# RWKV inverse in a two-layer hybrid block: its DRAM trips issued by ScalarE into ScalarE's own DMA queue

## The chip, the cores and the metric

The kernel runs on one core of one Trainium2 chip. The metric is the device time of one execution in microseconds, the median of three runs. TensorE multiplies (PE in the profile, its weight loads PEld), VectorE (DVE), ScalarE (ACT) and GpSimd (POOL) work element by element, and SyncE (SP) here only issues DMAs. DMAs that one engine issues go through a queue of that engine. Sixteen DMA engines move the data.

## The reference, cut to what matters

Two layers on 512 tokens of width 1024, each a half-step feed-forward, a mixer of three branches (retention, sparse attention, RWKV-7) merged by gates, and a second half-step feed-forward. The change touches the RWKV-7 branch alone, eight heads of 64, whose state is updated token by token:

```python
def step(S, inp):
    r_t, w_t, k_t, v_t, kk_t, a_t = inp
    sa = jnp.einsum('bhvk,bhk->bhv', S, -kk_t)
    S = S * w_t[:, :, None, :] + sa[..., None] * (kk_t * a_t)[:, :, None, :] + v_t[..., None] * k_t[:, :, None, :]
    return S, jnp.einsum('bhvk,bhk->bhv', S, r_t)
```

The kernel computes this in chunks of 64 tokens. In each chunk and head the dependence of later tokens on earlier ones is a triangular system (I - N) X = I of size 64, and its inverse is what the DRAM trips serve.

## The kernel before, in words

**Dense products.** A weight tile of 512 columns (a slot, 256 KB) is loaded by SP into `raw` (L54, four buffers), split by ACT into `whi` (L49) and by DVE into `wlo` (L50), three buffers each, and used by twelve matmuls of 512 columns, in three passes (L109, L111, L113). SP also moves saved tiles of 256 KB to and from DRAM (`th` at L863, `y` at L856, L908 and others), in the same queue.

**The mixer.** `Rwkv.pairs` walks through the four head pairs of a layer. For each pair `next` calls `front2` (decay, keys, operands `st` and `bk`) and `mid` (chunk products and inverse); `chain` then carries the state over eight chunks and `post` normalises. All of that is a serial chain with the highest priority, level `rec`. TensorE's time between its steps is filled by `K.fill(n, after)`: it traces n products of the queued dense work (retention, attention, gates, merging, the next pair's projections) and puts them, on TensorE, behind the instruction `after`. So the order on TensorE is mostly written out by hand: FV = 38 products behind `self.gate`, then the first small matmul `pace` (L470) that follows four steps of the inverse, then FP (11 to 15) products behind each further `pace`, FD = 29 behind the last, then the joining matmuls (L487, L492). The order on the other engines comes from a planner, which simulates the program's time and queues each instruction on its engine where it is ready. At run time every engine, and every DMA queue's issuer, takes its instructions in that fixed order and waits at the head of its line.

**The trips in `mid`.** (1) `zb` (L426, DVE, four parts) is the masked product. Its diagonal 32x32 blocks go to DRAM scratch `dn` in four DMAs (L456, 32 KB each, runs of 128 bytes). (2) One DMA (L457) brings `dn` back as `N`, one instance a partition, four times over (512 KB, the leading dimension of its source is a broadcast of four). (3) One DMA (L461) loads the start value `X` (`idg`, into buffer `cum`). (4) POOL runs 31 steps of two instructions (L466, L468). (5) X goes to DRAM scratch `dx` (L473) and comes back in four DMAs as `mt` (L479), is transposed by DVE into `m1` (L480), and the joining matmuls (L487) follow. There are eleven DMAs a pair and eight pairs, four in each layer.

Of the kernel before, what the change touches and what calls it, by code (L numbers as in the profile page):

```python
# [7 lines left out]
P = 128  # L8
# [6 lines left out]
T = 512  # L15
# [6 lines left out]
class Core:  # L22
# [17 lines left out]
    def ps(self, tag="f"):  # L40
        """one PSUM bank: d for the dense products, r for the recurrence, f for the rest."""
        return self.psp.tile([P, T], F32, tag=tag, name=self.nm("ps" + tag), bufs={"d": 4, "r": 2, "f": 2}[tag])
# [4 lines left out]
    def split(self, x, hi, lo):  # L47
        """exact parts of float32 for the one-pass products: x = hi + lo."""
        self.nc.scalar.activation(hi, x, AF.Copy)  # L49
        self.nc.vector.tensor_tensor(out=lo, in0=x, in1=hi.bitcast(F32), op=ALU.subtract)  # L50
# [6 lines left out]
    def wslot(self, src, n):  # L57
        """n <= 512 weight columns a partition, split."""
        raw = self.early.popleft() if self.early else self.load(src, n)
        hi = self.wp.tile([P, T], F32R, tag="whi", name=self.nm("whi"), bufs=3)  # L60
        lo = self.wp.tile([P, T], F32R, tag="wlo", name=self.nm("wlo"), bufs=3)
        with self.at("split"):
            self.split(raw[:, :n], hi[:, :n], lo[:, :n])
        return hi, lo

    @contextmanager
    def at(self, level):
        """what is traced here takes its place in that level of the scheduler's order."""
        s, self.tc.cur_priority = self.tc.cur_priority, self.level[level]
        yield  # L70
        self.level[level], self.tc.cur_priority = self.tc.cur_priority, s

    def fill(self, n=None, after=None):
        """trace n products of the queued work, on the tensor engine behind `after`; n None: all that is urgent."""
        with ExitStack() as es:
            es.enter_context(self.at("norm"))
            if after:
                es.enter_context(self.tc.issue_after(after.ins))
            while n != 0 and (self.urgent or n):
                g = self.urgent[0] if self.urgent and self.between else self.work  # L80
                try:
                    new = next(g)
                except StopIteration:
                    if g is self.work:
                        break
                    self.urgent.popleft()
                    continue
                if g is self.work:
                    self.between = new
                if new == "wait":  # L90
                    break
                if n and not new:
                    n -= 1
# [11 lines left out]
    def mm3(self, out, a, b, start, stop):  # L105
        """three passes: hi*hi + hi*lo + lo*hi; a is stationary."""
        nc = self.nc
        (ah, al), (bh, bl) = a, b
        nc.tensor.matmul(out, ah, bh, start=start, stop=False)  # L109
        yield  # L110
        nc.tensor.matmul(out, ah, bl, start=False, stop=False)  # L111
        yield
        nc.tensor.matmul(out, al, bh, start=False, stop=stop)  # L113
        yield

    def dense(self, w, x):
        """w [128, K, 128] in DRAM, x: K split chunks of the transposed input -> PSUM [128 features, 512 tokens]."""
        yield True
        pt = self.ps("d")
        n = len(x)  # L120
        for s0 in range(0, n, 4):
            nk = min(4, n - s0)
            hi, lo = self.wslot(w[:, s0:s0 + nk, :].rearrange("p k f -> p (k f)"), nk * P)
            for k in range(nk):
                f = slice(k * P, k * P + P)
                yield from self.mm3(pt, (hi[:, f], lo[:, f]), x[s0 + k], s0 + k == 0, s0 + k == n - 1)
        return pt

    def dense_tok(self, w, n, evac):
        """w [128, 8, n] in DRAM -> evac(token tile, PSUM [128 tokens, n features])."""  # L130
        yield True
        pts = [self.ps("d") for _ in range(4)]
        for k in range(KC):
            hi, lo = self.wslot(w[:, k, :], n)
            xh, xl = self.xg[k]
            for t in range(4):
                f = slice(t * P, t * P + P)
                yield from self.mm3(pts[t][:, :n], (xh[:, f], xl[:, f]), (hi[:, :n], lo[:, :n]), k == 0, k == KC - 1)
        for t in range(4):
            evac(t, pts[t][:, :n])  # L140
# [13 lines left out]
    def prep(self, x, c, gi, p):  # L154
        """chunk c of x^T -> split x*g, and its squares into the running sum."""
# [19 lines left out]
    def rstd(self, p, keep=True):  # L175
        """1/rms of each token: rs [128, 4] on the tokens' partitions, rb [128, 512] on every partition."""
# [17 lines left out]
    def ffn(self, xT, w_in, w_out, out_cb, done):  # L194
        """w_in [44, 128, 8, 128], w_out [8, 128, 22, 128]; x += 0.5 * swiglu, then out_cb(chunk)."""
        nc, tc = self.nc, self.tc
        with tc.tile_pool(name=self.nm("ffn"), bufs=1, reuse_waits="tile") as fp:
            tl = lambda tag, bufs=1, dt=F32: fp.tile([P, T], dt, tag=tag, name=self.nm(tag), bufs=bufs)
            act = []
            for j in range(NF):  # L200
# [6 lines left out]
                nc.gpsimd.tensor_tensor(out=u, in0=s, in1=u, op=ALU.mult)      # 2 * silu(g) * u  # L207
# [11 lines left out]
# columns of the rwkv parameter tile  # L219
MU, W0, A0, KK, KA, RK, LNW, LNB, NPAR = 0, 14, 18, 22, 26, 30, 34, 38, 42  # L220

# products traced behind the steps of a pair: its mixing products, the way to DRAM, four steps of the inverse, the way
# back, the joining of its blocks, each step of the chain, the chain; FM: behind no step
# [6 lines left out]
class Rwkv:  # L230
    """One layer's RWKV-7 branch, head pair by head pair (heads 2p at partitions 0-63, 2p+1 at 64-127)."""

    def __init__(self, K, pool, par, w2a2, g2, cst, y_out):
# [6 lines left out]
        # both low-rank factors: one's high parts at its rows, its low parts at the other's  # L240
# [9 lines left out]
        self.hwa = self.t("hwa", [P, 8])     # w0/2, a0/2  # L250
# [21 lines left out]
    def wide(self, h, ch):  # L272
        """columns ch of a low-rank factor's product with its half of la."""
        nc, s, z = self.nc, slice(64 * h, 64 * h + 64), self.K.ps("r")
        nc.tensor.matmul(z, self.wa[h][:, ch], self.lh[h], start=True, stop=False)
        nc.tensor.matmul(z, self.wa[h][s, ch], self.ll[s], start=False, stop=True)
        return z

    def shift(self, b, ps, out):
        """token shift of one projected block (still without its rstd) into out."""  # L280
# [25 lines left out]
    def front(self, p, blk):  # L306
        """projections of pair p; blk(b) gives the PSUM tile of projected block b."""
# [31 lines left out]
    def front2(self, p, r, k, v):  # L339
# [5 lines left out]
        # decay  # L345
# [15 lines left out]
        # in-context rate  # L361
# [6 lines left out]
        # normalised key  # L368
# [16 lines left out]
        # bonus  # L385
# [10 lines left out]
        # b (times -2)  # L396
# [12 lines left out]
    def mid(self, d):  # L409
        """chunk products, the triangular inverses, token-major operands."""  # L410
# [17 lines left out]
        with self.tc.issue_after(zl.ins):  # L428
            # token-major b|k and v
# [20 lines left out]
        # diagonal 32x32 blocks, one instance a partition  # L450
        dn = K.dram([4, 8, 32, 32], "dn", 2)
        N = self.t("N", [P, 32, 32])
        for h in range(2):
            for b in range(2):
                src = zb[64 * h + 32 * b:64 * h + 32 * b + 32, :, 64 * h + 32 * b:64 * h + 32 * b + 32]
                nc.sync.dma_start(dn[2 * h + b].rearrange("c s t -> s c t"), src)  # L456
        nc.sync.dma_start(N, dn.rearrange("b c s t -> (b c) s t")[None].to_broadcast([4, 32, 32, 32]))  # L457
        # X = (I - N)^-1; partition group g has the rows 4i+g
        X = self.t("cum", [P, 8, 32])
        tmp = self.t("E", [P, 8 * 31])  # L460
        nc.sync.dma_start(X, c["idg"])  # L461
# [11 lines left out]
        nc.sync.dma_start(dx.rearrange("b c (i g) t -> g (b c) i t", g=4), X)  # L473
        mt = d["mt"] = self.t("mt", [P, 8, 64])
        m1 = self.t("m1", [P, 8, 32])
        for h in range(2):
            a = 64 * h
            for b in range(2):
                nc.sync.dma_start(mt[a + 32 * b:a + 32 * b + 32, :, 32 * b:32 * b + 32], dx[2 * h + b].rearrange("c s t -> s c t"))  # L479
# [92 lines left out]
class Ret:  # L572
    """One layer's retention, two heads (a quarter) at a time; 128-token chunks are the token tiles."""
# [8 lines left out]
    def quarter(self, q, w):  # L582
        """w [128, 8, 512]: columns q (2x64), k (2x64), v (2x128)."""
# [28 lines left out]
    def heads(self, q, X, kd):  # L612
        K, nc, c = self.K, self.nc, self.c
        # states after chunks 0..2
# [60 lines left out]
class Dsa:  # L675
    """One layer's sparse attention: index scores, exact top-128, masked softmax over the causal keys."""
# [7 lines left out]
    def parts(self, pt, h, tag):  # L684
        """rows 64h.. of pt, split, on both halves of the partitions."""
# [9 lines left out]
    def stack(self, pt):  # L695
        """for each half of pt's rows, the high parts in their place and the low parts on the other half."""
# [10 lines left out]
    def dot(self, out, q, k, h):  # L707
        """q stacked (hi at half h), k in parts: hi*hi + lo*hi, then hi*lo."""
# [4 lines left out]
    def rope(self, x, nh, t):  # L713
        """first 16 of each head's 64 columns; x [128, nh, 64]."""
# [8 lines left out]
    def index(self, w):  # L723
        """w [128, 8, 452]: dk 64 | ki 64 | qi 256 | dv 64 | wi 4."""
# [52 lines left out]
    def attend(self, w):  # L777
        """w [128, 8, 512]: dq."""
# [12 lines left out]
        for qt in range(4):  # L791
# [6 lines left out]
            for b in range(4):  # L798
# [12 lines left out]
                # both heads' weights, transposed and split, against v's parts side by side  # L811
# [29 lines left out]
def gate(K, w, tl):  # L841
    """tanh(z / 2) and z of one gate block z."""
# [7 lines left out]
def gates(K, l, pool, a, yret, yg, thd):  # L850
    """the gated retention output, and tanh of the first len(thd) merge gates, to DRAM."""
# [14 lines left out]
def merge(K, l, pool, mh, a, yd, thd, rw):  # L866
    """sum over branches of sigmoid(gate) * (y @ p), times 2."""
# [159 lines left out]
def consts():  # L1027
# [19 lines left out]
    rel=p[None,:]-p[:,None]      # i - j, rows j  # L1047
# [9 lines left out]
def layout(i):  # L1057
    """the inputs re-laid for the chip: weights in tiles, vectors by partition, x transposed."""
# [39 lines left out]
```

## Time and profile before

| | us |
|---|---|
| median of 3 runs (lowest, highest) | 3109.18 (3108.01, 3110.92) |
| span of the profiled execution | 3103.6 |
| median less span | 5.6 |
| TensorE busy | 2990.3 (96%) |
| VectorE busy | 1761.8 (57%) |
| ScalarE busy | 1081.5 (35%) |
| GpSimd busy | 715.2 (23%) |

The span reaches from the first to the last instruction of one profiled execution. Busy time is a union of instructions, and a matmul's end is modelled. SP has no busy time in this profile: it only waits and issues.

### The profile page before, as it was taken

To read this page: it belongs to the slowest core of one execution; us is meant where nothing else is said; L and a number is where in the kernel's file an instruction comes from. 1 tells how busy PE (TensorE), PEld (TensorE's weight loads), DVE (VectorE), ACT (ScalarE), POOL (GpSimd) and SP (SyncE) were. 2 spreads that over 40 slices of the span, in tenths; PEclk is the share of its full clock that TensorE was granted. 3 is DMA by queue.
4 is the path that set the end of the run, shared out by engine and by line. 5 is a ranking of instruction groups with operands and counts; after the bars stand their busy time and mean duration, and the time that the engine had idled before them with its cause. 6 is when DMAs were issued, how large, how long until landed. Compare 5 with 4: busy or idle time off the path is not lost.

```text
span 3103.6 us, 40717 instructions
## 1 busy us (share of the span) xinstructions
PE 2990.3 (96%) x14336; PEld 2373.5 (76%) x14336; DVE 1761.8 (57%) x3641; ACT 1081.5 (35%) x1892; POOL 715.2 (23%) x1186
## 2 busy tenths in 40 slices
PE   9999999999899999999999999999999899999998
PEld 7888877767667778888888888677776677788886
DVE  5443388758675675443344433887585746644433
ACT  4333343334333233333333333433333333333322
POOL 2110024342433031111011101243423340311100
PEclk9999999999899999999999999899999999999999
DMA  4223422223223452233322234222333135523232
GB/s 136 98 97 106 117 72 70 73 85 124 81 85 96 139 190 95 95 99 94 97 95 97 98 109 118 66 72 71 96 110 92 64 110 155 175 92 99 96 95 89
DMA packets 203580, 314.08 MB, mean 101 GB/s; under 512 B 46320, under 2 KB 60400, under 8 KB 203376
## 3 DMA queue, kind: packets, MB, share of 16 engines
q1 hardware_dynamic: 203376, 311.49, 32.2%
q8 instruction: 112, 1.84, 0.2%
q14 instruction: 92, 0.75, 0.1%
HBM read 277.86 MB, written 33.55 MB: 100 GB/s over the span
## 4 chain that ended last, share of the span: by engine, by line
PE 74%; DVE 10%; POOL 6%; DMA 6%; issue 3%; ACT 1%; SPq 0%; DVEq 0%; POOLq 0%; ACTq 0%
PE psd L113 22%; PE psd L109 22%; PE psd L111 22%; DMA N<-dn 3%; POOL cum L468 2%; POOL E L466 2%; DVE wlo L50 2%; PE psr L421 1%; DMA th<-th 1%; PE psr L504 1%; PE psf L96 1%; DMA dx<-cum 1%; DMA y<-y 1%; DVE cb L523 1%; PE psr L514 1%
## 5 line engine op out<-in xcount | busy, mean ns | idle before, releaser
L49 ACT ACTIVATE whi<-raw 128x512 fp32r<-128x512 f32 (+2 forms) x920 | 571.5, 622 | 1259.6 <-PE psd L111 927.2
L50 DVE TENSOR_TENSOR wlo<-raw,whi 128x512 fp32r<-128x512 f32 (+2 forms) x920 | 657.6, 715 | 560.0 <-ACT whi L49 543.9
L111 PE MATMUL psd<-xl,whi 128*128 128x512 f32 x2144 | 856.0, 399 | 2.4 <-DVE xl L161 2.4
L109 PE MATMUL psd<-xh,whi 128*128 128x512 f32 x2144 | 850.6, 397 | 1.5 <-DVE g L203 1.5
L113 PE MATMUL psd<-xh,wlo 128*128 128x512 f32 x2144 | 849.9, 396 | 0.1
L111 PEld LDWEIGHTS psd<-xl,whi 128*128 128x128 f32 x2144 | 406.7, 190 | 88.9 <-DVE xl L161 4.4
L109 PEld LDWEIGHTS psd<-xh,whi 128*128 128x128 f32 x2144 | 406.6, 190 | 88.5 <-issue 3.4
L113 PEld LDWEIGHTS psd<-xh,wlo 128*128 128x128 f32 x2144 | 406.9, 190 | 84.1 <-issue 1.4
L207 POOL TENSOR_TENSOR u<-s,u 128x512 f32<-128x512 f32 x88 | 141.2, 1605 | 841.0 <-DVE u L206 726.3
L109 PE MATMUL psd<-ah,whi 128*128 128x512 f32 x704 | 277.4, 394 | 0.0
L113 PE MATMUL psd<-ah,wlo 128*128 128x512 f32 x704 | 276.0, 392 | 0.0
L111 PE MATMUL psd<-al,whi 128*128 128x512 f32 x704 | 273.2, 388 | 0.0
L172 POOL TENSOR_TENSOR sq<-sq,sq 128x512 f32<-128x512 f32 x42 | 56.1, 1336 | 467.4 <-ACT sq L170 467.4
L113 PE MATMUL psd<-whi,xl 128*128 128x512 f32 (+1 forms) x384 | 160.6, 418 | 0.0
L111 PE MATMUL psd<-wlo,xh 128*128 128x512 f32 (+1 forms) x384 | 156.1, 407 | 0.0
L113 PEld LDWEIGHTS psd<-ah,wlo 128*128 128x128 f32 x704 | 132.1, 188 | 31.0
L109 PE MATMUL psd<-whi,xh 128*128 128x512 f32 (+1 forms) x384 | 155.1, 413 | 0.0
L111 PEld LDWEIGHTS psd<-al,whi 128*128 128x128 f32 x704 | 132.2, 188 | 29.6
L109 PEld LDWEIGHTS psd<-ah,whi 128*128 128x128 f32 x704 | 132.3, 188 | 26.3
L50 DVE TENSOR_TENSOR al<-u,ah 128x512 fp32r<-128x512 f32 x88 | 61.8, 702 | 153.6 <-ACT ah L49 153.4
L206 DVE TENSOR_TENSOR u<-psd,rb 128x512 f32<-128x512 f32 x88 | 60.9, 692 | 127.3 <-PE psd L113 127.3
L810 POOL TENSOR_SCALAR L<-L,mx 128x128 f32<-128x128 f32 (+3 forms) x64 | 71.4, 1118 | 199.4 <-DVE mx L809 99.0
(262 smaller groups left out, 3907.2 us busy)
## 6 DMA issues: line engine op xcount, KB each, us to landing
raw<-in_wf_dram SPq DMA_DIRECT2D x184, 256.0 KB
raw<-in_ffa_in_dram SPq DMA_DIRECT2D x176, 256.0 KB
raw<-in_ffb_in_dram SPq DMA_DIRECT2D x176, 256.0 KB
th<-th SPq DMA_DIRECT2D x96, 256.0 KB
raw<-in_ffa_out_dram SPq DMA_DIRECT2D x80, 256.0 KB
raw<-in_wt_dram SPq DMA_DIRECT2D x80, 256.0 KB
raw<-in_ffb_out_dram SPq DMA_DIRECT2D x80, 256.0 KB
x<-x SPq DMA_DIRECT2D x32, 256.0 KB
```

The source lines that it names most:

```text
L49: self.nc.scalar.activation(hi, x, AF.Copy)
L50: self.nc.vector.tensor_tensor(out=lo, in0=x, in1=hi.bitcast(F32), op=ALU.subtract)
L96: return self.nc.tensor.transpose(out, x, self.ident)
L109: nc.tensor.matmul(out, ah, bh, start=start, stop=False)
L111: nc.tensor.matmul(out, ah, bl, start=False, stop=False)
L113: nc.tensor.matmul(out, al, bh, start=False, stop=stop)
L172: nc.gpsimd.tensor_tensor(out=sq, in0=sq, in1=self.ssq[0], op=ALU.add)
L206: nc.vector.tensor_tensor(out=u, in0=pu, in1=self.rb, op=ALU.mult)
L207: nc.gpsimd.tensor_tensor(out=u, in0=s, in1=u, op=ALU.mult) # 2 * silu(g) * u
L466: nc.gpsimd.tensor_tensor(out=tv, in0=X[:, 0:n, u:u + 1].to_broadcast([P, n, w]), in1=N[:, u:u + 1, u + 1:].to_broadcast([P, n, w]), op=AL ...
L468: nc.gpsimd.tensor_tensor(out=X[:, 0:n, u + 1:], in0=X[:, 0:n, u + 1:], in1=tv, op=ALU.add)
L810: nc.gpsimd.tensor_scalar(out=x, in0=x, scalar1=mx[:, 3:4], scalar2=None, op0=ALU.mult)
```

## The change

The eleven DMAs of the trips in `mid` are issued by ScalarE instead of SyncE. Nothing else is computed or moved differently. The diff also takes out comments and docstrings; they are cut here.

```diff
@@ mid
         for h in range(2):
             for b in range(2):
                 src = zb[64 * h + 32 * b:64 * h + 32 * b + 32, :, 64 * h + 32 * b:64 * h + 32 * b + 32]
-                nc.sync.dma_start(dn[2 * h + b].rearrange("c s t -> s c t"), src)
-        nc.sync.dma_start(N, dn.rearrange("b c s t -> (b c) s t")[None].to_broadcast([4, 32, 32, 32]))
+                nc.scalar.dma_start(dn[2 * h + b].rearrange("c s t -> s c t"), src)
+        nc.scalar.dma_start(N, dn.rearrange("b c s t -> (b c) s t")[None].to_broadcast([4, 32, 32, 32]))
         X = self.t("cum", [P, 8, 32])
         tmp = self.t("E", [P, 8 * 31])
-        nc.sync.dma_start(X, c["idg"])
+        nc.scalar.dma_start(X, c["idg"])
...
         dx = K.dram([4, 8, 32, 32], "dx", 2)
-        nc.sync.dma_start(dx.rearrange("b c (i g) t -> g (b c) i t", g=4), X)
+        nc.scalar.dma_start(dx.rearrange("b c (i g) t -> g (b c) i t", g=4), X)
...
             for b in range(2):
-                nc.sync.dma_start(mt[a + 32 * b:a + 32 * b + 32, :, 32 * b:32 * b + 32], dx[2 * h + b].rearrange("c s t -> s c t"))
+                nc.scalar.dma_start(mt[a + 32 * b:a + 32 * b + 32, :, 32 * b:32 * b + 32], dx[2 * h + b].rearrange("c s t -> s c t"))
```

## Rows read from the trace of the kernel before

**Rows 1.** The page: busy time of each engine, and the chain by line.

```profile
PE 2990.3 (96%) x14336; PEld 2373.5 (76%) x14336; DVE 1761.8 (57%) x3641; ACT 1081.5 (35%) x1892; POOL 715.2 (23%) x1186
...
PE psd L113 22%; PE psd L109 22%; PE psd L111 22%; DMA N<-dn 3%; POOL cum L468 2%; POOL E L466 2%; DVE wlo L50 2%; PE psr L421 1%; DMA th<-th 1%; PE psr L504 1%; PE psf L96 1%; DMA dx<-cum 1%; DMA y<-y 1%; DVE cb L523 1%; PE psr L514 1%
```

**Rows 2.** Windows, first mixer stretch: length, busy of each engine, clock, DMA share, GB/s.

```profile
350.00:1100.00 750.00, 707.58 (x3701) 539.47 (x3701) 508.28 (x1250) 271.69 (x505) 236.09 (x512) 0.95 0.31 96
```

**Rows 3.** Waits, whole span: total us, times, longest us.

```profile
POOL E L466 <- DMA N<-dn: 59.9, 7, 12.0
...
PE psr L470 <- POOL cum L468: 25.4, 14, 4.9
...
PEld psr L487 <- DVE m L480: 3.8, 7, 1.1
```

**Rows 4.** Timeline of TensorE at the first pace: start, us, [idle before <-releaser].

```profile
472.96 0.19 PE L470 MATMUL psr<-ident,cum 128*1 128x1 f32 x2 [2.34 <-POOL cum L468]
...
825.43 0.55 PE L96 MATMUL psf<-ident,L 128*128 128x128 f32 x3 [3.07 <-POOL L L810]
...
2508.41 0.19 PE L470 MATMUL psr<-ident,cum 128*1 128x1 f32 x2 [2.59 <-POOL cum L468]
```

**Rows 5.** Timeline of SP in the second pair, both trips.

```profile
641.85 0.80 SPq L456 DMA_DIRECT2D dn<-zb  x2
643.91 0.56 SPq L457 DMA_DIRECT2D N<-dn  x1
644.57 7.25 SPq L54 DMA_DIRECT2D raw<-in_wf_dram  x3
...
688.72 0.56 SPq L473 DMA_DIRECT2D dx<-cum  x1
...
693.49 1.80 SPq L479 DMA_DIRECT2D mt<-dx  x4
```

**Rows 6.** Timeline of DVE in the second pair, behind the way back.

```profile
695.22 0.43 DVE L480 STREAM_TRANSPOSE m<-mt 32x256 f32<-32x256 f32 x1 [4.58 <-DMA mt<-dx]
...
696.78 0.69 DVE L50 TENSOR_TENSOR wlo<-raw,whi 128x512 fp32r<-128x512 f32 x1
```

**Rows 7.** Timeline of POOL in the second pair, the inverse's first instruction.

```profile
654.69 0.24 POOL L466 TENSOR_TENSOR E<-cum,N 128x31 f32<-128x31 f32 x1 [11.34 <-DMA N<-dn]
```

**Rows 8.** Windows while N flows in the second pair; columns as in Rows 2.

```profile
646.00:647.00 1.00, 1.00 (x8) 0.84 (x7) 0.00 (x0) 0.90 (x3) 0.00 (x0) 1.00 0.86 250
...
650.50:652.00 1.50, 1.50 (x16) 1.34 (x16) 1.23 (x3) 0.24 (x1) 0.00 (x0) 1.00 0.24 71
...
653.60:655.60 2.00, 0.13 (x1) 0.00 (x0) 0.00 (x0) 0.00 (x0) 0.72 (x3) 1.00 0.21 73
```

**Rows 9.** Timeline of SP in the third pair, the trip to POOL.

```profile
808.43 1.16 SPq L456 DMA_DIRECT2D dn<-zb  x2
...
811.25 0.55 SPq L457 DMA_DIRECT2D N<-dn  x1
...
816.51 5.26 SPq L54 DMA_DIRECT2D raw<-in_wf_dram  x3
```

**Rows 10.** Waits of SP's queue, whole span: total us, times, longest us.

```profile
SPq L461 <- DVE bk L403: 37.4, 8, 7.2
SPq L456 <- DVE zb L426: 27.3, 16, 4.0
SPq L473 <- POOL cum L468: 25.8, 8, 4.3
...
SPq L479 <- DMA dx<-cum: 14.7, 8, 1.9
```

**Rows 11.** Timeline of ACT in the second pair, around both trips.

```profile
642.78 0.63 ACT L49 ACTIVATE whi<-raw 128x512 fp32r<-128x512 f32 x1 [0.80 <-PE psd L113]
...
691.39 0.63 ACT L49 ACTIVATE whi<-raw 128x512 fp32r<-128x512 f32 x1 [1.44 <-PE psd L111]
```

**Rows 12.** Window behind the second pair's first pace; columns as in Rows 2.

```profile
658.00:662.00 4.00, 3.97 (x13) 3.12 (x14) 0.80 (x1) 1.32 (x2) 3.18 (x10) 0.63 0.02 4
```

## The prediction, made before the changed kernel was run

> **What bounds the kernel now.** The page comes first: TensorE is busy for 96% of the span, and three quarters of the chain that ended last are dense matmuls, with the trip N<-dn as its largest item that is neither a matmul nor another engine's work, 3% [rows 1]. So a change pays only where it removes idle or slow time of TensorE, and costs where it adds some. The windows by stage say where such time is: in the first mixer stretch TensorE is busy for 707.6 of 750 us at a mean granted clock of 0.95 [rows 2]; the second layer's mixer looks the same. The waits then name what a DRAM trip is to TensorE: POOL sits idle 59.9 us in all for N, and TensorE 25.4 us in 14 waits for POOL's inverse [rows 3]. Most of that falls at the first pace of each pair. The timeline shows 2.34 us in the first pair and 2.59 in the last [rows 4]; in the third and seventh pair the stall stands on a transposition (3.07 us) whose POOL instruction is queued behind the one that waits for N. The eight add up to 26.2 us. They are the only idle time of TensorE that a faster way to N could take away, and a slower way adds to them one for one: 38 products stand between the gate and the pace, they have run out, and what is filled in next is traced behind the pace.
>
> **How fast the trip is.** The issues are not late today: SP stands at dn before zb is done (27.3 us in 16 waits), at dx before POOL is done (25.8 in 8), and at mt before dx has landed (14.7 in 8) [rows 10]. In the second pair the last dn writes are issued at 641.85, N at 643.91, and POOL starts at 654.69 [rows 5, 7]: about 2.1 us for the write, 10.8 for the read back. The write takes that in the second pair and three others, 2.3 in three, and 2.8 in the third [rows 9], where a load stands ahead of it. The read takes 10.1 us in the first pair, 10.8 here and 12.0 in the fifth. On the way out dx is issued at 688.72, mt at 693.49, and the transposition starts at 695.22 [rows 5, 6]; L487 stands right at the edge behind it (3.8 us of PEld waits, seven times) [rows 3].
>
> **Part 1: dn leaves the weights' queue.** What can be gained is the excess over 2.1 us, 0.7 in the third pair and 0.2 in three, 1.3, and some tenths where SP was busy with a load as dn landed: together 2 us off the stalls. I take -2, bounds -5 and 0.
>
> **Part 2: N leaves the weights' queue.** While N flows alone, the DMA share is 0.24 and the rate 71 GB/s [rows 8]: four of sixteen engines, and those full, since the same engines add up to 0.86 when a load is spread over all. 512 KB at 71 GB/s are 7.4 us, which is most of the 10.8. A load that SP issues after N stands behind it on these four engines; the last row of the group shows it, 73 GB/s for 2 us more after N's last bytes, though the last of the three loads [rows 5] was issued at 651.5. In a queue of its own N loses that protection: the loads' quarter, 64 KB each, is moved among N's data. At 71 GB/s that is 0.92 us for each load. Three such loads are issued while N flows in the second pair [rows 5], four in the third (the first two of the three at its end among them [rows 9]); over the eight pairs I count 1, 3, 4, 3, 3, 3, 4 and 3, that is 24 or 22 us. The bounds are 0 (the loads still come after N) and 22. I take 15, nearer the upper end because the four engines are full and the last load in each pair shares only in part. In return the loads land sooner, which I cost at nothing: TensorE does not wait for a split here, and the tiles are loaded several slots ahead into four buffers. The Trainium skill says the same of the queues (DMA: Bandwidth & Descriptors, Queues, rings and completion order): each DMA engine goes round the queues that have work, one packet at a time. No row of this kernel has two busy queues, so the trace can't confirm it; by that rule alone the term would be 22.
>
> **Part 3: the issues go to ScalarE.** Each pair puts eleven issues there, by SP's durations 0.3 to 0.56 us each (0.8 for two dn, 0.56 for N and for dx, 1.8 for four mt [rows 5]), about 4.8 us a pair with idg, 38 us in all on an engine with 35% busy time: it has room. Two delays are possible. First, a trip waits for what ACT runs at its head. When the last dn is due, at 641.85, the next split on ACT waits for TensorE until 642.78 and a copy follows it [rows 11]. Behind nothing this costs 0, behind one activation 0.63, behind a split that waits up to 2.1 us. Over the 16 half-trips the bounds are 0 and about 20 us; ACT is idle at most of the moments and the trips have the highest priority, so I take 0.3 each, 5 us. Second, ACT inherits SP's waits: 37.4 us for bk, 27.3 for zb, 25.8 for POOL's end, 14.7 for dx [rows 10], 105 us. Queued behind them are the splits and the activations of attention. The splits have cover: in the second pair whi is split at 691.39, but its wlo only at 696.78, since DVE stands at mt [rows 6, 11], so 4 us on ACT are free there; and elsewhere around the trips a slot's split ends 2 to 10 us ahead of its first matmul (the ends of L50 against the starts of L109). I cost this at 0; without the cover a third to a half of the 40 us behind L473 and L479 would reach TensorE, about 15.
>
> **Part 4: what SP gains.** SP no longer stops for 105 us [rows 10], so loads go out a little sooner. TensorE waits for none of them: 0.
>
> **Part 5: the clock.** Behind the first stall of the second pair the clock is 0.63 over 4 us [rows 12], that is, about 3 us at 1.2 GHz instead of 2.4; six of the eight first stalls have such a stretch, worth about 1.7 us each, the first pair's has none. Longer stalls would give the first pair its stretch and lengthen one or two: +3, bounds 0 and 8.
>
> **The sum.** -2 + 15 + 5 + 0 + 3 = +21 us. The profiled span is 3103.6 and the median 5.6 above it; 3124.6 + 5.6 is 3130.
>
> **The rivals.** (a) **Nothing moves.** The four engines take N first anyway or have room, the issues cost nothing, and the trip is as long as before: -2 to +5, so 3107 to 3114. For it speaks that SP delayed no dn or N issue; against it that the four engines are full. The Trainium skill has a rule to this effect (DMA: Bandwidth & Descriptors, Issuing engines are not separate DMA queues): issuing from several engines saves only the issuing time. By it SP's 38 us of issue go, which bound nothing, and 3109 stays. (b) **Faster.** N starts and flows at once in its own queue, and lands 2 us sooner in every pair, for instance because the loads that slow it now without standing ahead of it (10.1 us in the first pair with one, 12.0 in the fifth with three) are spread otherwise, or because the planner places the waiting POOL instructions better. 16 us of stall go, and three or four slow stretches with them, 6: 3087. It decides from the point at which N takes under 9 us from issue to POOL's start. Against it: full engines and an issue that was never late. (c) **Much slower.** The planner puts a waiting trip ahead of attention's activations on ACT, or a trip behind a waiting split, in most pairs: the 15 us of part 3 without cover, and the 20 instead of 5: 3130 + 30 = 3160. It decides where a trip's issue is later than its data by over 1 us. That the DMAs don't move to another queue is not a case: they are issued by a different engine by name.
>
> **How the numbers follow.** My forecast, N delayed and small delays on ACT (3116 to 3145), has 0.50; (c) 0.15; (a) 0.20; (b) 0.15. The likeliest is 3130. The bounds of the terms reach from 3104 (-5, 0, 0, 0) to 3159; the range 3100 to 3160 leaves out most of (b) and a part of (c). A measurement here tells apart some 0.2%, 6 us: faster by more than that 0.15, within it 0.20, slower 0.65.
>
> **What would show it.** Right: N from issue to POOL's first step 12 to 14 us in pairs with three or four loads and unchanged in the first; a DMA share near 0.9 all along N's flow and no tail behind it; first stalls of 4 to 7 us; a second queue on the page. Part 3: dn issued over 0.1 us after zb, and ACT idle at L49 until dx or POOL. Wrong: N's trip below 11 us everywhere, or first stalls as before while the time changes; then it is the order on DVE, ACT or POOL that moved, and this working has no term for it.

## The result: slower by what was forecast, in another place

The changed kernel takes 3127.1 us (median of 4 runs, 3125.8 to 3130.8); the kernel before, beside it, 3108.6 (3107.0 to 3110.9). The ratio is 1.006, its 95% interval 1.0046 to 1.0073: 18.5 us slower, where +21 was forecast. The profiled execution has a span of 3125.9 us (before 3103.6).

The page of the changed kernel: the engines' busy time, and the DMA queues (packets, MB, share of sixteen engines).

```profile
PE 3001.5 (96%) x14336; PEld 2381.8 (76%) x14336; DVE 1757.4 (56%) x3641; ACT 1078.1 (34%) x1892; POOL 714.1 (23%) x1186
...
q1 hardware_dynamic: 175536, 303.10, 31.5%
q10 hardware_dynamic: 27840, 8.39, 1.2%
```

The trips did move to a second queue, q10. TensorE is busy 11 us longer for the same 14336 matmuls [rows 1], so part of the loss is slower matmuls, not idle time. Now the views that the prediction named. First the waits of the changed kernel (total us, times, longest us):

```profile
POOL E L466 <- DMA N<-dn: 46.8, 6, 11.8
...
ACT whi L49 <- DMA mt<-dx: 31.5, 5, 8.9
...
PE psr L470 <- POOL cum L468: 26.6, 18, 4.5
```

POOL's wait for N is 7.8 us each time, against 8.6 before [rows 3]; TensorE's wait for the inverse has grown by 1.2 us in all. POOL's waits depend on what else POOL has to do, but the trips themselves say the same: from N's issue to POOL's first step they take 9.7 to 11.9 us, before 10.1 to 12.0, and not the 12 to 14 of the prediction. N is not later. What is new is the middle row, ScalarE held at the issue of `mt` until `dx` has landed (and while it issues). TensorE's timeline at the first paces tells the same:

```profile
471.33 0.19 PE L470 MATMUL psr<-ident,cum 128*1 128x1 f32 x2 [2.47 <-POOL cum L468]
...
827.89 0.55 PE L96 MATMUL psf<-ident,L 128*128 128x128 f32 x3 [2.44 <-POOL L L810]
...
2528.54 0.19 PE L470 MATMUL psr<-ident,cum 128*1 128x1 f32 x2 [2.58 <-POOL cum L468]
```

2.47, 2.44 and 2.58 us, where it was 2.34, 3.07 and 2.59 [rows 4]: the first stalls are as before; all eight together are 24.5 us, against 26.2. The prediction says what that means: not the trips, but an order has moved.

**Where the time goes.** Lay the two traces beside each other step by step. The fourth pair's chain of layer 1 (L504, the step that carries the state) starts at 1018.0 us in both. The next feed-forward (its first L206) starts at 1203.0 before and at 1222.4 after. In the timelines of TensorE and VectorE, before:

```profile
1018.01 0.66 PE L504 MATMUL psr<-sv,stk 128*128 128x64 f32 x4
...
1202.96 0.68 DVE L206 TENSOR_TENSOR u<-psd,rb 128x512 f32<-128x512 f32 x1
```

After:

```profile
1017.97 0.55 PE L504 MATMUL psr<-sv,stk 128*128 128x64 f32 x4
...
1222.41 0.68 DVE L206 TENSOR_TENSOR u<-psd,rb 128x512 f32<-128x512 f32 x1
```

So 19.5 us are lost between these two points, 3.3 in the same stretch of layer 2, and nothing that stays before, between or behind. The windows of that stretch, first before, then after (length, busy time of PE, PEld, DVE, ACT, POOL, granted clock, DMA share, GB/s):

```profile
1018.00:1060.00 42.00, 39.37 (x212) 29.97 (x210) 26.20 (x73) 13.72 (x23) 3.24 (x10) 0.88 0.49 158
1060.00:1203.00 143.00, 138.60 (x631) 110.31 (x630) 90.40 (x154) 49.43 (x81) 35.05 (x25) 1.00 0.48 151
```

```profile
1018.00:1060.00 42.00, 35.76 (x180) 25.15 (x178) 24.68 (x90) 8.68 (x19) 9.04 (x16) 0.62 0.12 39
1060.00:1203.00 143.00, 136.27 (x581) 107.08 (x581) 88.82 (x134) 51.73 (x85) 33.24 (x22) 0.98 0.55 173
```

During the chain TensorE idles 6.2 us instead of 2.6, its mean granted clock is 0.62 instead of 0.88, and DMA moves 39 GB/s instead of 158: there is hardly any dense work that needs weights. A clock of 0.62 is 2.4 GHz for a quarter of the time and 1.2 for the rest. As an estimate from these windows, the loss is 3.6 us of idle time and 42 x 0.26 = 10.9 of clock, then 2.3 and 143 x 0.02 = 2.9 in the second window: 19.7 for the 19.5.

What is missing shows in the groups of TensorE's instructions at 1017 to 1060 us, first before, then after:

```profile
L109 PE MATMUL psd<-yh,whi 128*128 128x512 f32 x25 | 10.4, 443 | 0.0
...
L824 PE MATMUL psf<-X,v 128*128 128x256 f32 x4 | 1.1, 305 | 0.3 <-DVE X L50 0.3
```

```profile
L824 PE MATMUL psf<-X,v 128*128 128x256 f32 x10 | 4.5, 454 | 0.5 <-DVE X L50 0.5
...
L109 PE MATMUL psd<-xh,whi 128*128 128x512 f32 x7 | 2.7, 391 | 0.0
```

`psd<-yh` is the merge of the branches, a third of its products (L111 and L113 have as many). Before, 75 of them run beside the chain; after, none, and of the dense products only 21 of the gates (`psd<-xh` and its two partners). L823 and L824 are attention's last products: 4 of each are left at the chain's start before, 10 after. The order in which TensorE takes its products is written into the program, so this is the program's order and not a delay at run time: counted in the two traces, 3026 of the 14336 matmuls stand at another place than before. And the merge can't start while attention runs: in `mixer` the pool `mrg` opens only when the pool `dsa` has been closed, on the same side of the memory. That is read from the code; TensorE's timeline agrees, before and after:

```profile
1030.36 0.28 PE L824 MATMUL psf<-X,v 128*128 128x256 f32 x1
...
1036.84 0.77 PE L109 MATMUL psd<-yh,whi 128*128 128x512 f32 x1
```

```profile
1055.90 0.41 PE L824 MATMUL psf<-X,v 128*128 128x256 f32 x1
...
1061.96 1.22 PE L109 MATMUL psd<-yh,whi 128*128 128x512 f32 x2
```

6 us from attention's last product to the merge's first, both times; only that attention ends 12.6 us behind the chain's start before, and 38.4 after. In between the gates' products run out (after, the last is at 1024 us), and the chain's small matmuls (64 columns, serial with DVE) are alone with attention's.

### The profile page after: what moved, and what is told of

Same layout as the page of the kernel before. It is cut to its first block, busy times and chain, and to the rows that moved or that the text cites. A ratio compares the mean times of both kernels' runs of the same rounds, so it can differ in the third digit from the quotient of the medians.

```text
span 3125.9 us, 40685 instructions
## 1 busy us (share of the span) xinstructions
PE 3001.5 (96%) x14336; PEld 2381.8 (76%) x14336; DVE 1757.4 (56%) x3641; ACT 1078.1 (34%) x1892; POOL 714.1 (23%) x1186
## 3 DMA queue, kind: packets, MB, share of 16 engines
q1 hardware_dynamic: 175536, 303.10, 31.5%
## 4 chain that ended last, share of the span: by engine, by line
PE 77%; DVE 9%; DMA 6%; POOL 5%; issue 3%; ACT 1%; SPq 0%; ACTq 0%; DVEq 0%; POOLq 0%
PE psd L113 23%; PE psd L109 22%; PE psd L111 22%; DMA N<-dn 3%; POOL E L466 2%; POOL cum L468 2%; DVE wlo L50 2%; PE psr L421 1%; DMA dx<-cum 1%; PE psr L504 1%; DMA th<-th 1%; PE psf L96 1%; PE psf L652 1%; PE psr L514 1%; DMA y<-y 1%
## 5 line engine op out<-in xcount | busy, mean ns | idle before, releaser
L111 PE MATMUL psd<-xl,whi 128*128 128x512 f32 x2144 | 855.7, 399 | 2.1 <-DVE xl L161 2.1
L113 PE MATMUL psd<-xh,wlo 128*128 128x512 f32 x2144 | 850.8, 397 | 0.1
L111 PEld LDWEIGHTS psd<-xl,whi 128*128 128x128 f32 x2144 | 406.4, 190 | 88.8 <-DVE xl L161 3.8
L113 PEld LDWEIGHTS psd<-xh,wlo 128*128 128x128 f32 x2144 | 406.9, 190 | 84.4 <-issue 2.3
L113 PE MATMUL psd<-ah,wlo 128*128 128x512 f32 x704 | 276.0, 392 | 0.0
L111 PE MATMUL psd<-al,whi 128*128 128x512 f32 x704 | 273.2, 388 | 0.0
L113 PE MATMUL psd<-whi,xl 128*128 128x512 f32 (+1 forms) x384 | 160.0, 417 | 0.0
L111 PE MATMUL psd<-wlo,xh 128*128 128x512 f32 (+1 forms) x384 | 156.3, 407 | 0.0
L113 PEld LDWEIGHTS psd<-ah,wlo 128*128 128x128 f32 x704 | 132.1, 188 | 30.9
L111 PEld LDWEIGHTS psd<-al,whi 128*128 128x128 f32 x704 | 132.2, 188 | 29.6
L206 DVE TENSOR_TENSOR u<-psd,rb 128x512 f32<-128x512 f32 x88 | 60.8, 691 | 127.6 <-PE psd L113 127.6
```

What stands on the lines that cost most here:

```text
L206: nc.vector.tensor_tensor(out=u, in0=pu, in1=self.rb, op=ALU.mult)
```

## The theories

**Order theory:** the eleven issues changed what the planner wrote down for TensorE. Attention's last head-pair blocks stand some 12 products later behind the pairs of layer 1; the merge is late by them, the fourth chain runs without dense products, and the clock falls. The queue itself costs little. **Queue theory:** the trips' new queue, or ScalarE held at their issues, costs the 18 us, and the tail (the stretch from the fourth pair's chain to the next feed-forward) is only where it surfaces.

All runs are set beside the kernel before, run with them on the same chip (its medians there were 3107.2 to 3110.1); the columns on the tails are worked out from each profiled trace: L is the time from the first L504 of a layer's fourth pair to the end of its last L824, T that from the same L504 to the next feed-forward's first L206. They are from one profiled run of each kernel, and runs of one kernel, with one order, spread by up to 15 us: the profiled runs of e2, e6 and e7 lie 7, 6 and 3 us above their medians, that of e8 5 below.

| kernel | us (median) | ratio, 95% interval | layer 1: L, T | layer 2: L, T |
|---|---|---|---|---|
| before | 3108.6 | 1 | 12.6, 185.0 | 12.6, 184.3 |
| after | 3127.1 | 1.0060 (1.0046 to 1.0073) | 38.4, 204.4 | 15.8, 187.6 |
| e1: after, FV 37 | 3119.9 | 1.0032 (1.0020 to 1.0044) | 16.8, 189.2 | 17.8, 189.5 |
| e2: before, FV 37 | 3113.8 | 1.0013 (1.0004 to 1.0023) | 15.6, 186.1 | 29.1, 197.5 |
| e3: eleven moved, layer 1 only | 3126.1 | 1.0044 (1.0031 to 1.0057) | 37.7, 206.1 | 11.8, 182.6 |
| e4: eleven moved, layer 2 only | 3113.0 | 1.0013 (1.0004 to 1.0021) | 12.6, 185.6 | 15.7, 188.6 |
| e5: nothing moved, one block late | 3123.5 | 1.0045 (1.0033 to 1.0057) | 34.0, 203.0 | 12.6, 186.2 |
| e6: dn and N moved | 3112.7 | 1.0010 (1.0000 to 1.0020) | 16.6, 190.6 | 12.2, 183.4 |
| e7: dx and mt moved | 3114.1 | 1.0016 (1.0007 to 1.0025) | 13.1, 183.7 | 11.1, 183.5 |
| e8: after, mt back on SyncE | 3111.6 | 1.0005 (0.9996 to 1.0013) | 15.9, 188.2 | 11.9, 182.6 |
| e9: before, N in four | 3062.7 | 0.9854 (0.9839 to 0.9869) | 12.6, 185.0 | 12.6, 185.1 |
| e10: after, N in four | 3078.3 | 0.9903 (0.9886 to 0.9920) | 15.0, 189.4 | 12.3, 184.6 |
| e11: dx, mt moved, N in four | 3072.5 | 0.9891 (0.9875 to 0.9908) | 13.1, 185.2 | 13.1, 184.7 |
| e12: dn, N moved, N in four | 3076.8 | 0.9906 (0.9891 to 0.9921) | 15.5, 186.5 | 15.5, 187.3 |

Read the two right columns down: where attention ends 11 to 18 us behind the chain's start, the tail takes 183 to 191 us; where it ends 29 to 38 behind it, 198 to 206, whichever queue the trips are in. The last entry of e2 is the kernel before with one number changed.

## Experiments: the order or the queue

**The one that moves no DMA (e5).** One block of attention in layer 1 is traced at the lower level `late`:

```diff
-                L = [self.t("L", bufs=2) for _ in range(2)]
+                e = K.at("late" if (K.layer, qt, b) == (0, 3, 1) else "norm"); e.__enter__(); L = [self.t("L", bufs=2) for _ in range(2)]
...
-                self.y_out(qt, b, y)
+                self.y_out(qt, b, y); e.__exit__(None, None, None)
```

> No DMA is moved: the kernel before, with one head-pair block of attention in layer 1 (query tile 3, block 1) traced at the level late, which puts TensorE's order behind the fourth pair where the changed kernel has it: 61 attention products ahead of the chain instead of 72, 72 at its middle instead of 80, and 3264 dense products at its last step instead of 3362. Order theory: the loss of layer 1 without any new queue, 3122 to 3131 us, with 30 us or more of half clock in the chain of the fourth pair. Queue theory: 3106 to 3113 us.

Measured: 3123.5 us, +14.1 with nothing moved out of SyncE's queue. Its window over the chain, and then attention's group at 1017 to 1060 us:

```profile
1018.00:1060.00 42.00, 34.99 (x176) 24.62 (x175) 26.45 (x95) 9.20 (x19) 9.01 (x16) 0.58 0.16 49
```

```profile
L824 PE MATMUL psf<-X,v 128*128 128x256 f32 x10 | 4.5, 452 | 0.3 <-DVE X L50 0.2
```

Clock 0.58 and 49 GB/s, ten of L824 left: the picture of the changed kernel. The order alone makes a tail of 203.0 us, 18 more than before. The queue theory's 3106 to 3113 falls.

**The order mended, the queue kept (e1, control e2).** In e1 all eleven DMAs stay on ScalarE and one product fewer is traced behind the gate; e2 is the same edit in the kernel before.

```diff
-FZ, FV, FD, FB, FE = 11, 38, 29, 5, 46
+FZ, FV, FD, FB, FE = 11, 37, 29, 5, 46
```

> All eleven DMAs of the trip stay in ScalarE's queue as in the changed kernel; only the count of dense products traced behind the way to DRAM goes from 38 to 37 (FV), which puts the last head-pair blocks of attention on TensorE ahead of the fourth pair's chain of layer 1 again, as in the kernel before. Order theory (the loss is TensorE's order behind the fourth pair): 3104 to 3113 us, so 0.999 to 1.001 of before, with under 15 us of half clock at 1025 to 1070 us. Queue theory (the trips' new queue, or ScalarE's waits, cost the 18 us): 3123 to 3132 us.

> The kernel before with FV 37 instead of 38 and nothing else: what that one number is worth with the trips in SyncE's queue. Both theories: 3104 to 3114 us; the order theory needs it within 0.3% of before, or the first run's gain could be that of the number alone.

Measured: 3119.9 and 3113.8. The first lies between the two theories' ranges and misses both; the second is at the upper edge of its range. The window over the chain in e1:

```profile
1018.00:1060.00 42.00, 38.48 (x200) 28.01 (x200) 24.36 (x68) 13.93 (x26) 5.83 (x10) 0.84 0.42 131
```

The merge is back beside the chain (131 GB/s, clock 0.84) and layer 1's tail is 189.2 instead of 204.4. But FV 37 costs 3.7 us by itself: in e2's order attention is late in layer 2 (8 of L824 left at the chain's start instead of 4). With that one order its runs spread from 3106 to 3121, and the profiled one is the slowest, so its 197.5 is at the upper end. Against that control 6 us are left to the moved trips, of the changed kernel's 18.5. Two thirds of the loss go with FV 37; since it moves products at many other places too, this pair alone is no proof.

**Which DMAs (e8, e6, e7).** Each takes `nc.scalar` for the lines named and `nc.sync` for the others; e8 is the changed kernel with

```diff
-                nc.scalar.dma_start(mt[a + 32 * b:a + 32 * b + 32, :, 32 * b:32 * b + 32], dx[2 * h + b].rearrange("c s t -> s c t"))
+                nc.sync.dma_start(mt[a + 32 * b:a + 32 * b + 32, :, 32 * b:32 * b + 32], dx[2 * h + b].rearrange("c s t -> s c t"))
```

> The changed kernel with the four loads of mt back on SyncE; dn, N, idg and dx, the waiting store of 0.6 to 2.2 us, stay on ScalarE. The order behind the fourth pair is that of before again. Order theory: 3106 to 3115 us. Queue theory (seven of the eleven DMAs, N and dx among them, still moved): 3118 to 3127 us.

> Only the way out is moved to ScalarE's queue: the four stores of dn and the load of N (40 of 88 DMAs; N is the transfer that the first stalls wait for); idg, dx and mt stay on SyncE. TensorE's order behind the fourth pair stays that of before. Order theory: 3106 to 3114 us. Queue theory (N unprotected against the weights' loads): most of the loss, 3119 to 3128 us, with a longer wait of the inverse for N.

> Only the way back is moved to ScalarE's queue: the store of dx and the four loads of mt. TensorE's order behind the fourth pair stays that of before. Order theory: 3106 to 3114 us. Queue theory (ScalarE's instructions wait behind dx and mt): 3114 to 3122 us.

Measured: e8 3111.6 (+2.2, not to be told from no change), e6 3112.7 (+3.3), e7 3114.1 (+4.7, at the upper edge of the order theory's range and the lower edge of the other's). In e8 seven of eleven DMAs are still ScalarE's, N and `dx` among them:

```profile
1018.00:1060.00 42.00, 38.18 (x196) 29.22 (x196) 25.59 (x71) 13.31 (x23) 4.86 (x11) 0.84 0.46 141
```

Neither half moves attention far by itself (L 16.6 and 13.1), and the costs of the halves, 3.3 and 4.7, don't add up to 18.5. That is a step in a schedule, not a price per DMA. e8 alone would not part the theories, since it also frees ScalarE of `mt`. e7 does: there ScalarE is held for `mt<-dx` 21.3 us in three times, attention is on time, and 4.7 us are lost, not 18. Its interval, 2 to 8 us, leaves a small true cost of the way back.

**Which layer (e3, e4).**

```diff
-        self.gate, self.done = None, False
+        self.gate, self.done, self.q = None, False, K.nc.scalar if K.layer == 0 else K.nc.sync
...
-        nc.sync.dma_start(N, dn.rearrange("b c s t -> (b c) s t")[None].to_broadcast([4, 32, 32, 32]))
+        self.q.dma_start(N, dn.rearrange("b c s t -> (b c) s t")[None].to_broadcast([4, 32, 32, 32]))
```

and so for the other ten; e4 has `K.layer == 1`.

> The eleven DMAs go to ScalarE's queue in layer 1 alone; in layer 2 they stay on SyncE. Order theory: attention is late behind the fourth pair of layer 1 as in the changed kernel, so 3104 + 19 = 3121 to 3130 us. Queue theory: half of the trips, so half of the loss, 3115 to 3120 us.

> The eleven DMAs go to ScalarE's queue in layer 2 alone. Order theory: layer 1's order is that of before, layer 2's tail costs about 3 us: 3108 to 3114 us. Queue theory: half of the loss, 3115 to 3120 us.

Measured: 3126.1 and 3113.0. Layer 1 carries 16 of the 18.5 us, layer 2 2.9. Both have the same trips; they differ in that attention is late in layer 1 alone (L 37.7 against 15.7).

## Experiments: the price of N's trip

The prediction rests on each microsecond of N's trip being one of the kernel's. e9 tests that with the load of N in four DMAs, one for each group of 32 partitions, so that no leading dimension of four holds it to a quarter of the DMA engines:

```diff
-        nc.sync.dma_start(N, dn.rearrange("b c s t -> (b c) s t")[None].to_broadcast([4, 32, 32, 32]))
+        [nc.sync.dma_start(N[32 * g:32 * g + 32], dn.rearrange("b c s t -> (b c) s t")) for g in range(4)]
```

> The price of N's trip by itself: the kernel before with the load of N issued as four DMAs of 32 partitions instead of one broadcast DMA, so that its 512 KB aren't drawn by four DMA engines alone; everything stays on SyncE and TensorE's order is that of before. If the first stalls behind N cost the end one to one, as the prediction says: N lands in some 5 us instead of 10.4, most of the 26 us of first stalls go, 3080 to 3095 us. If other work covers N's trip: 3106 to 3112 us.

Measured: 3062.7 us, 45.6 less than the kernel before beside it; this kernel beats both. Two views of it: a window in the second pair, with the second half of N and the start of the load behind it, and the waits:

```profile
642.50:644.50 2.00, 2.00 (x15) 1.69 (x14) 0.55 (x1) 1.71 (x3) 0.00 (x0) 1.00 0.89 245
```

```profile
POOL E L466 <- DMA N<-dn: 16.9, 7, 5.6
PEld psr L470 <- POOL cum L468: 14.3, 28, 1.3
PE psr L470 <- POOL cum L468: 5.5, 9, 1.1
```

POOL's waits for N and TensorE's for the inverse (the rows of POOL and PE) are a third of those before and less [rows 3]. The DMA share is 0.89, the rate 245 GB/s, where N alone had 0.24 and 71 [rows 8]. From the first issue to the last landing a trip takes 4.4 us instead of 10.8 (means of eight, to the last report of landing): 51 us shorter in all, and 45.6 come out at the end. The Trainium skill (DMA: Bandwidth & Descriptors, Rules for kernel authors) says that a leading zero-stride broadcast of c copies confines the whole DMA to at most c engines; these rows agree.

e10 is the changed kernel with the same edit on ScalarE; e11 and e12 split it (e11 moves only `dx` and `mt`, e12 only `dn` and N).

> The changed kernel (all eleven on ScalarE, then fourteen) with the same four DMAs for N; TensorE's order behind the fourth pair comes out on time (72 attention products ahead of its chain, 80 at its middle). Order theory: within 6 us of the kernel before with N in four, on either side. Queue theory (the weights' loads interleave with N, or ScalarE's waits cost): 10 us or more above it.

> N in four DMAs on SyncE; only the way back (dx and the four loads of mt) is on ScalarE's queue. Of TensorE's 13066 instructions 209 stand at another place than in the kernel with N in four and everything on SyncE; GpSimd's order is the same. This splits the 15.6 us by which the run with all on ScalarE stood above that kernel. Order theory (the rest too is TensorE's order, which here hardly differs): 3061 to 3066 us. Queue theory (later dx and mt, ScalarE held): 3067 to 3075 us.

> N in four DMAs, and only the way out (the four stores of dn, the four loads of N) on ScalarE's queue; dx and mt on SyncE. 2063 of TensorE's 13066 instructions stand at another place, from the first pair of layer 1 on. Order theory: nearly all of the 15.6 us, 3072 to 3080 us, lost in small gaps and in the clock behind them and not in the way out itself, whose wait for N stays within 5 us in all of that of the kernel with N in four on SyncE. Queue theory: 3066 to 3072 us, and the wait for N longer by about as much.

Measured: 3078.3, 3072.5 and 3076.8. Here the order theory fails as it was put: e10 stands 15.6 us above e9, not within 6, and of the 17.7 us between their profiled spans only 4.4 lie in layer 1's tail. e11 is in the queue theory's range. Its reason can be read in ScalarE's timeline in the first pair, and in the windows behind it, of e9 and then e11:

```profile
497.30 1.10 ACTq L473 DMA_DIRECT2D dx<-cum  x1
502.10 1.86 ACTq L479 DMA_DIRECT2D mt<-dx  x4
504.01 0.72 ACT L286 ACTIVATE v<-P,omm 128x512 f32<-128x512 f32 x1 [8.12 <-issue]
504.64 0.61 ACT L49 ACTIVATE whi<-raw 128x512 fp32r<-128x512 f32 x1
```

```profile
505.00:545.00 40.00, 40.00 (x247) 30.33 (x247) 38.03 (x103) 14.06 (x24) 7.83 (x17) 1.00 0.26 82
```

```profile
505.00:545.00 40.00, 39.42 (x227) 29.93 (x225) 32.93 (x86) 13.38 (x24) 5.48 (x11) 0.87 0.21 65
```

ScalarE runs nothing for 8.12 us: it issues `dx`, stands some 4 us until that has landed, and issues `mt` for 1.9; a projection's copy and two splits are queued behind it. In the 40 us behind it TensorE runs 89 dense products where e9 runs 107, with more small ones of retention, and its clock is 0.87 where e9 has 1.00. In the profiled runs this pair's chain loses 5.8 of the 12.1 us between e9 and e11. A late attention is not the reason: the tails are as in e9 (185.2 and 184.7), and 247 of TensorE's 14336 matmuls stand at another place. That the hold causes the rest too was not tried.

e12's 14 us lie in the order theory's range, and POOL's wait for N stays within 5 us of e9's, as that theory asked (18.1 against 16.9). But the trip does grow: from first issue to last landing N takes 5.3 us in ScalarE's queue (5.4 in e10), against 4.4 and 4.3 in SyncE's (e9 and e11), 7 us more over eight pairs. TensorE's wait for the inverse follows it: 10.3 us in e12 and 9.5 in e10, against 5.5 in e9 and 3.9 in e11. So with short trips the queue has a price of some us; how the 14 divide between order and queue stays open.

## Why the prediction was right in size and wrong in cause

**What bounds the kernel** held: waits for N cost the end nearly one for one (45.6 of 51 us, e9). The cap was wrong. "The only idle time that a faster way to N could take away" was put at 26.2 us. That much goes in e9, where no first stall is left: TensorE idles 26 us less. The clock came on top: it is 0.975 over 3103.6 us before and 0.980 over 3059.5 in e9, so 33 us less at 1.2 GHz, worth 16, and TensorE is busy 18 us less. 26 + 18 are the 44 between the two profiled spans.

**Part 1** (-2): no gain. From the last `dn` issue to N's takes 15.3 us over eight pairs before and 15.9 after.

**Part 2** (+15) is the step that failed. It has N delayed by 15 us because loads in another queue take turns with it. From issue to landing N takes 86.5 us over eight pairs before and 86.4 after; 88.5 in e6, 88.8 in e8, 89.4 in e1. In the kernels with N in one DMA on SyncE it is 86.5 (before), 85.2 (e2), 86.5 (e5) and 88.5 (e7). The means of four and four are 88.3 and 86.7, so the term is about 2 us, not 15. The quarter of a load did not interleave with N piece by piece: in the changed kernel a 256 KB transfer that SP issues within 9 us behind N takes 5.8 us to land (median of 27; 6.7 to 7.0 in e1, e6 and e8), against 7.0 with N in the same queue; over the whole kernel a load takes 2.6. So the loads mostly still came after N, and no share near 0.9 stood all along its flow: in the second pair it is 0.25 from 650 to 652 us. The Trainium skill's rule (DMA: Bandwidth & Descriptors, Queues, rings and completion order) was read too finely: it says that an engine drains a whole packet, typically 9 to 17 descriptors, from one ring before it turns to the next. I took a packet for one small piece. If a quarter of N were few packets, the rule could fit the 5.8; how many they are no row shows.

**Part 3** (+5, and 0 for the inherited waits). The issues were hardly late: `dx` goes out 0.03 us behind POOL's last step in all eight pairs, before and after, and `dn` is 0.2 to 0.4 us late three times of sixteen. What did grow is the way back. From the issue of `dx` to DVE's transposition it takes 52.3 us over eight pairs before and 57.1 after; in all kernels with `dx` on SyncE 52.0 to 52.7 (e2, e5, e6, e9, e12 too), in those with `dx` in ScalarE's queue 54.3 to 57.1 (e1, e7, e8, e10, e11 too). So 2 to 5 us are there, but as a slower trip and not as a late issue; why the trip is slower no run shows. The inherited waits did hold the splits, 31.5 us in five times, and cover hid them here, since nothing was lost up to the fourth chain. With shorter trips the cover fails at least in the first pair (e11, 5.8 of the 12.1 us between its profiled span and e9's): the "about 15 without cover" was the right worry at the wrong kernel.

**Part 4** (0): nothing speaks against it, and no run tests it alone. **Part 5** (+3 for longer first stalls): the stalls did not grow, but the slow stretches behind them did. The first pair's, which the prediction expected, is there: its clock is 0.57 from 471 to 475 us, where it was 1.00 at the same step before (473 to 477). All eight together are 34 us instead of 27, worth 3 (before, seven pairs had one, not six). Nothing of that is left at the start of the fourth chain. The clock's larger share of the loss, 14 us, lies in the tail, for which the prediction had no term.

**The missing term** is the one the text named last as its way of being wrong: an order that moved, on TensorE itself. The prediction costed instructions where they stood, though the planner places every one anew when the cost of an engine changes. The tail of the fourth chain was never looked at as a place with no slack; 19.5 + 3.3 us there are the whole of the 22.3 us between the profiled spans. Rival (c) spoke of the planner, but of ScalarE's order around the trips. Why the planner puts attention later when `mt` is ScalarE's beside the way out, and doesn't with either half alone, is not settled: only that it does, and that putting `mt` back (e8) undoes it. That a sum of +21 with no term for this came within 3 us of +18.5 is luck.

## What to carry to other kernels

When a planner places the work, an edit of issue engines is also an edit of every engine's order: compare the two kernels' progress at the same landmarks (which filler is still left when a serial chain starts) before costing a queue. Look for the stretch where the filler ends and what gates the next supply; here one head-pair block of attention ahead of a memory pool was worth 14 to 18 us. And look at how many DMA engines a transfer uses before asking which queue it stands in: that was worth two and a half to three times as much (45.6 us, e9).

## What the runs showed of the hardware

- A 512 KB load on four DMA engines was hardly slowed by 256 KB loads on sixteen in another queue: N took 11.0 us a trip beside them (mean of four kernels) and 10.8 with the loads queued behind it, and a transfer issued behind N still took 5.8 to 7.0 us instead of 2.6. Spread over all engines, N took 5.3 and 5.4 us in ScalarE's queue (e12, e10) and 4.4 and 4.3 in SyncE's (e9, e11).
- In the changed kernel's fourth chain TensorE ran only 64-column steps and attention's products from 1027 to 1060 us; it was busy 84% of that time, at a granted clock of 0.51. Before, from 1041.3 to 1060 us, it ran the same steps with the merge's 512-column products between them, was busy throughout, and had a clock of 1.00.
- An issue that waits for a DMA stopped everything behind it on ScalarE: up to 8.9 us at once in the changed kernel, 31.5 in five times.
